# Value passes over other PSUM banks, an eighth place for attention outputs, and loads moved between two DMA queues, in a two-network kernel

## The chip, the cores and the metric

The kernel runs on one core of one Trainium2 chip. The time is device microseconds of one execution, the median of the runs that are shown. Four compute engines have queues of their own and run in the order written for each: TensorE (PE, matrix products into PSUM, with its weight loads shown as PEld), VectorE (DVE), ScalarE (ACT) and GpSimd (POOL). SyncE (SP) issues transfers only. A transfer (DMA) can be issued on the queue of SP or on that of POOL. An instruction that waits holds up everything behind it in its own queue.

## What is computed

A network of two layers (`first_block`) and then a second one (`second_block`), on 512 tokens of width 1024, all in float32. The change touches the first network only. Each of its layers is, cut to what matters:

```python
h = rms_norm(x, g_mix[l])
c_q, c_kv, k_r, qkv_b, qkv_c, gate_logits = jnp.split(h @ w_in[l], IN_SPLITS, axis=-1)
y_a = mla_mixer(c_q, c_kv, k_r, ...)                       # 8 heads, keys and values from a rank-128 latent
y_b = dilated_mixer(rope(q_b), rope(k_b), v_b)             # 3 groups of 4 heads; the groups' outputs are
                                                           # merged with softmax(lse) as weights
y_c = neighbourhood_mixer(q_c, k_c, v_c, rpb[l])           # 8 heads, each looks at a window, with a bias table
gates = sigmoid(gate_logits)
merged = gates[0] * (y_a @ w_pa) + gates[1] * (y_b @ w_pb) + gates[2] * (y_c @ w_pc)
x = x + merged @ w_o[l]
h = rms_norm(x, g_ffn[l])
x = x + (silu(h @ w1[l]) * (h @ w3[l])) @ w2[l]
```

## The kernel before

**Products.** Every float32 operand is split into a high and a low part (`split`, L245: ACT writes the high part at L248, or L251 where there is a scale; DVE the low part at L249 or L252), and a product is three matmuls (`mm3`, L264; in the trace L266 to L268). A weight tile is loaded on SP's queue into `wst` (two places) and split into `whi` and `wlo` (three places each; `weights`, L255).

**PSUM.** Eight banks under four names (L1576): `mm` 3, `S` 2 (attention scores), `T` 2 (transposed probabilities), `O` 1 (attention outputs). Names rotate over their own places, so a product into a bank waits until the readers of its last tenant are done.

**Two streams woven.** Attention is written as short steps (`attn_pair`, L318: scores, transposes at L363, products with the values at L404, and DVE's addition of the two halves at L414, for two heads, a "head pair", at a time). `weave` (L458) puts between these steps a second stream of dense work, the fill, as much of it as the steps' costs times a ratio ask for. The order that results is fixed when the program is built.

**First stage of a layer** (0 to 136 us and 1003 to 1120 us of the trace). `latent` (L771) makes the latent queries and keys, pauses twice (L807 and L817, by the numbers in `PAUSE`, which count fill), takes two column sums with `ones_sum` and roots them (`inv_root`: ACT's square root, then DVE's reciprocal; `rcol` turns the second into columns `rc3`), and writes the latent values to DRAM (`vda`). Its fill is `v_tokens` (L713), the values of all other heads: two passes of 32 products 512 wide and a third 256 wide. The first two take the banks T, T, S, S, and the third two halves of each T. Each result goes out by `v_store` (L740): ACT and DVE scale and split it into `vn`, of which there are two places, and POOL issues the store of `vn` (L743). A layer has 28 such stores, 20 of values and 8 of latent values.

**Attention** (136 to 560 us and 1110 to 1540 us). Fourteen pairs: four latent, then six dilated (three groups of two), then four of neighbourhood attention (nb, units `u` 0 and 1 of two pairs). `v_load` (L745) fetches a pair's values from DRAM into `V` (two places), with one to eight transfers on POOL's queue (L753; eight for nb). An output is collected in a tile `O` of a pool of six places (`obufs`, L1578), which is also used for other tiles of that size. `stat_rows` writes a group's maxima and denominators through a small tile `row` or `row8` to DRAM. After the third dilated group `dil_merge` (L937) loads them (`st`, L940), computes the merge weights, writes these to DRAM (`fd`, L956), loads them back spread over partitions (`RD`, two places, twelve transfers on POOL's queue, L961) and multiplies the six dilated outputs by them (DVE, L963) and adds them up (POOL, L965). Only then are the places of four of these six outputs free.

**The end of attention.** Finished outputs go to DRAM as `yd` and come back by `load_split` (L593: a load on POOL's queue, L595, then a split). The fill of the last nb unit is `first_outputs` (L600) and `first_products` (L614), which multiplies the latent and the dilated outputs by their weights. After the stream, `early_outputs` (L1016) loads and splits the outputs of nb unit 0, and the loop at L651 multiplies all four nb outputs by `wpc`, with `m` and `t` loaded from DRAM (`ry` and `gate`, two places each).

Of the kernel before, what the change touches and what calls it, by code (L numbers as in the profile page):

```python
# [20 lines left out]
S = 512  # L21
# [14 lines left out]
W1 = 2.0  # L36
PAUSE = ((11000, 8000), (9000, 11500))
# [174 lines left out]
class _Net:  # L212
# [105 lines left out]
    def attn_pair(self, scores, nk, mask, v, order, rq=None, wide=False, pre=None, post=None):  # L318
# [9 lines left out]
        def score(j, g):  # L328
            if j == 0 and g == 0:
                c["nmx"] = self.t(self.tp, "nmx", (P, 2, 4), bufs=3)  # L330
                c["den"] = self.t(self.tp, "den", (P, 2, 4), bufs=3)
                c["o"] = self.t(self.tp, "O", (P, S), bufs=self.obufs)
# [166 lines left out]
    def stat_rows(self, stat, order, dst):  # L499
# [3 lines left out]
        if len(order(ps).shape) == 2:  # L503
            nc.tensor.transpose(ps[0:8, 0:P], stat.rearrange("p j b -> p (j b)"), self.ident)
            row = self.t(self.tp, "row8", (8, P), bufs=1)
# [5 lines left out]
        row = self.t(self.tp, "row", (2, S), bufs=1)  # L511
# [54 lines left out]
    def first_layer(self, l, acc, xsrc, emit_x):  # L566
        nc, a = self.nc, self.a
        with ExitStack() as lctx:
# [45 lines left out]
            def first_products():  # L614
# [7 lines left out]
                for n in range(8):  # L622
                    t = self.t(self.tp, "gate", (P, S), bufs=2)
# [18 lines left out]
            with ExitStack() as actx:  # L642
# [70 lines left out]
    def v_tokens(self, win, rc, vd):  # L713
# [3 lines left out]
        for base, units, width, per in ((24, (0, 1), 512, 2), (28, (2, 3), 512, 2), (32, (4,), 256, 4)):  # L717
            if width == 512:
                ps = [self.bank(x) for x in "TTSS"]
            else:  # L720
                ps = [bk[:, i * 256:i * 256 + 256] for bk in [self.bank(x) for x in "TT"] for i in range(2)]
                w = [self.weights(win[base + c]) for c in range(2)]
            for k in range(8) if width == 512 else ():
                if k % per == 0:
                    w = self.weights(win[base + k // per])
                o = slice(k % per * width, (k % per + 1) * width)
# [3 lines left out]
            for tk in range(4):  # L730
                for k in range(8) if width == 256 else ():
                    o = slice(k % per * width, (k % per + 1) * width)
                    self.mm3(ps[tk], self.hh[:, k, sl[tk]], self.hl[:, k, sl[tk]], w[k // per][0][:, o], w[k // per][1][:, o],
                             k == 0, k == 7)
                    yield 330
                for i, u in enumerate(units):
# [918 lines left out]
```

## Time and profile before

| | us |
|---|---|
| median of 3 runs | 2542.53 (2536.6 to 2544.38) |
| profiled execution | 2536.82, its span 2535.0, mean granted TensorE clock 0.962 |
| PE busy | 2366.3 (93% of the span) |
| DVE, ACT, POOL busy | 1571.8 (62%), 1174.7 (46%), 797.8 (31%) |
| first layer, second layer | about 0 to 1005 and 1005 to 1960 |
| second network | about 1960 to 2535 |

The page of the profile gives these shares first, then the span in 40 slices, then the transfers. The granted clock is 1.0 where TensorE runs at 2.4 GHz and 0.5 where it runs at 1.2 GHz; a mean between the two says how the stretch was divided. A wait is put down to the instruction that released it. A line of code can be that of a helper: L248, L249, L266 to L268 are used everywhere, so the name of the tile tells which work it is.

### The profile page before, as it was taken

To read this page: it belongs to the slowest core of one execution; us is meant where nothing else is said; L and a number is where in the kernel's file an instruction comes from. 1 tells how busy PE (TensorE), PEld (TensorE's weight loads), DVE (VectorE), ACT (ScalarE), POOL (GpSimd) and SP (SyncE) were. 2 spreads that over 40 slices of the span, in tenths; PEclk is the share of its full clock that TensorE was granted. 3 is DMA by queue.
4 is the path that set the end of the run, shared out by engine and by line. 5 is a ranking of instruction groups with operands and counts; after the bars stand their busy time and mean duration, and the time that the engine had idled before them with its cause. 6 is when DMAs were issued, how large, how long until landed. Compare 5 with 4: busy or idle time off the path is not lost. (4 is left out here: it accounts for less than half of the span.)

```text
span 2535.0 us, 31781 instructions
## 1 busy us (share of the span) xinstructions
PE 2366.3 (93%) x11200; PEld 1945.8 (77%) x11200; DVE 1571.8 (62%) x2387; ACT 1174.7 (46%) x2072; POOL 797.8 (31%) x953
## 2 busy tenths in 40 slices
PE   7799998789999999889999788999999899979995
PEld 5688887578888888678888577878888788858884
DVE  6477796566444333567878566676533667697666
ACT  5366675344323223356767343423222366435653
POOL 3225466623111100224547633211112122142214
PEclk9899999799999999989999799999999999989997
DMA  5455556556333344355647455687434332224222
GB/s 169 157 174 147 166 143 187 135 175 209 111 99 93 96 130 133 133 172 160 179 127 192 142 157 183 220 282 230 133 109 151 110 109 81 84 91 121 73 78 75
DMA packets 140462, 362.13 MB, mean 143 GB/s; under 512 B 29744, under 2 KB 37200, under 8 KB 140304
## 3 DMA queue, kind: packets, MB, share of 16 engines
q1 hardware_dynamic: 101456, 275.72, 35.5%
q0 software_dynamic: 38848, 84.39, 11.7%
q8 instruction: 88, 1.44, 0.2%
q14 instruction: 70, 0.57, 0.1%
HBM read 286.78 MB, written 45.86 MB: 131 GB/s over the span
## 5 line engine op out<-in xcount | busy, mean ns | idle before, releaser
L248 ACT ACTIVATE whi<-wst 128x1024 fp32r<-128x1024 f32 (+4 forms) x387 | 374.1, 967 | 712.6 <-PE mm L267 256.8
L249 DVE TENSOR_TENSOR wlo<-wst,whi 128x1024 fp32r<-128x1024 f32 (+4 forms) x387 | 460.6, 1191 | 299.7 <-ACT whi L248 291.8
L266 PE MATMUL mm<-hh,whi 128*128 128x512 f32 x1184 | 470.6, 397 | 11.6 <-ACT whi L248 9.0
L268 PE MATMUL mm<-hh,wlo 128*128 128x512 f32 x1184 | 467.2, 395 | 0.5 <-DVE wlo L249 0.3
L267 PE MATMUL mm<-hl,whi 128*128 128x512 f32 x1184 | 465.4, 393 | 0.0
L266 PEld LDWEIGHTS mm<-hh,whi 128*128 128x128 f32 x1184 | 224.1, 189 | 54.2 <-ACT whi L248 9.6
L268 PEld LDWEIGHTS mm<-hh,wlo 128*128 128x128 f32 x1184 | 223.5, 189 | 49.5 <-DVE wlo L249 2.7
L267 PEld LDWEIGHTS mm<-hl,whi 128*128 128x128 f32 x1184 | 224.1, 189 | 43.2 <-issue 0.2
L697 POOL TENSOR_TENSOR s<-s,rf 128x512 f32<-128x512 f32 x44 | 75.8, 1724 | 400.4 <-ACT s L696 400.4
L363 PE MATMUL T<-ident,E 128*128 128x128 f32 x768 | 119.8, 279 | 7.3 <-DVE pl L249 2.8
L339 PE MATMUL S<-qk,qk 128*128 128x512 f32 (+2 forms) x512 | 114.1, 340 | 12.7 <-ACT E L351 6.5
L534 POOL DMA_DIRECT2D ry<-tmp x136 | 67.9, 506 | 168.3 <-ACT tmp L531 109.5
L248 ACT ACTIVATE ph<-T 128x512 fp32r<-128x512 f32 x160 | 95.0, 596 | 53.1 <-PE T L363 49.3
L363 PEld LDWEIGHTS T<-ident,E 128*128 128x128 f32 x768 | 94.8, 143 | 27.7 <-DVE pl L249 4.0
L249 DVE TENSOR_TENSOR pl<-T,ph 128x512 fp32r<-128x512 f32 x128 | 87.3, 683 | 21.9 <-ACT ph L248 21.3
L339 PEld LDWEIGHTS S<-qk,qk 128*128 128x128 f32 x512 | 80.7, 195 | 25.3 <-ACT E L351 8.5
L415 POOL TENSOR_TENSOR O<-O,ll 64x256 f32<-64x256 f32 x80 | 73.5, 919 | 72.1 <-DVE O L414 70.1
L300 POOL TENSOR_TENSOR tmp<-tmp,tmp 128x512 f32<-128x512 f32 x26 | 42.4, 1630 | 170.6 <-ACT tmp L296 159.5
L348 ACT ACTIVATE E<-E,nmx 128x256 f32<-128x256 f32 (+1 forms) x160 | 72.8, 456 | 47.3 <-DVE nmx L346 46.9
L266 PE MATMUL S<-hh,whi 128*128 128x512 f32 x208 | 82.0, 394 | 5.3 <-ACT hh L251 5.3
L268 PE MATMUL S<-hh,wlo 128*128 128x512 f32 x208 | 81.8, 393 | 1.3 <-DVE wlo L249 1.3
L267 PE MATMUL S<-hl,whi 128*128 128x512 f32 x208 | 82.0, 394 | 0.4 <-DVE hl L252 0.4
(626 smaller groups left out, 5595.2 us busy)
## 6 DMA issues: line engine op xcount, KB each, us to landing
wst<-win SPq DMA_DIRECT2D x153, 512.0 KB, 4.0
wst<-w SPq DMA_DIRECT2D x120, 512.0 KB, 3.6
mw<-wada SPq DMA_DIRECT2D x48, 512.0 KB, 4.5
td<-gate SPq DMA_DIRECT2D x48, 256.0 KB, 3.1
vd<-vn POOLq DMA_DIRECT2D x40, 256.0 KB, 2.3
qk<-qk POOLq DMA_DIRECT2D x80, 128.0 KB, 3.1
V<-vd POOLq DMA_DIRECT2D x80, 128.0 KB, 6.4
ry<-tmp POOLq DMA_DIRECT2D x136, 64.0 KB, 3.9
```

The lines of the kernel that those rows point to most:

```text
L248: nc.scalar.activation(hi, src, AF.Copy)
L249: nc.vector.tensor_tensor(lo, src, hi.bitcast(F32), op=ALU.subtract)
L266: mm(out, ah, bh, start=start, stop=False, **kw)
L267: mm(out, ah, bl, start=False, stop=False, **kw)
L268: mm(out, al, bh, start=False, stop=stop, **kw)
L300: self.nc.gpsimd.tensor_tensor(new, acc, sq, op=ALU.add)
L339: nc.tensor.matmul(sp[:, i * nk:(i + 1) * nk], a, b, start=n == 0, stop=n == len(ops) - 1)
L348: nc.scalar.activation(e[:, sl], e[:, sl], AF.Exp, scale=-1.0, bias=m, accum_out=d)
L363: nc.tensor.transpose(tp[:, i * P:(i + 1) * P], e[:, i * P:(i + 1) * P], self.ident)
L415: nc.gpsimd.tensor_tensor(dst, dst, lo, op=ALU.add)
L534: nc.gpsimd.dma_start(out=y[r:r + 32], in_=f[r ^ 32:(r ^ 32) + 32])
L697: nc.gpsimd.tensor_tensor(s, s, r, op=ALU.mult)
```

## The change

Seven edits, all in the first network:

1. **Value passes.** The first pass takes the banks mm, mm, mm, T, the second T, S, S, O, the third two halves of one `mm` bank for each two token tiles. The latent values take `mm` only, where they alternated between `mm` and `O`. `rc` is passed as a function, so that it is looked up when a store needs it.
2. **Pauses and ratio.** `PAUSE` is (31000, 10000) for both layers, and `W1` 1.0 where it was 2.0.
3. **Output places.** `obufs` is 7 where it was 6, and the first dilated output of a layer lies in a place of its own outside that pool (`spare`, the tag `accf`): eight in all. `row8` and `row` become one tile.
4. **Value loads** (`v_load`) are issued on SP's queue, not POOL's: 50 transfers in a layer.
5. **Loads of finished outputs** (`load_split`) too: 8 in a layer.
6. **Last splits in the fill.** `early_outputs` runs inside `first_products`, ahead of its seventh of eight rounds, not after the stream.
7. **Merge loop.** `m` is taken from `tmp` (4 places) and `t` from `O` (7 places).

```diff
-W1 = 2.0
-PAUSE = ((11000, 8000), (9000, 11500))
+W1 = 1.0
+PAUSE = (31000, 10000)
...
-                c["o"] = self.t(self.tp, "O", (P, S), bufs=self.obufs)
+                c["o"] = home() if home else self.t(self.tp, "O", (P, S), bufs=self.obufs)
...
-            row = self.t(self.tp, "row8", (8, P), bufs=1)
+            row = self.t(self.tp, "row", (8, self.roww), bufs=1)[:, 0:P]
...
-        row = self.t(self.tp, "row", (2, S), bufs=1)
+        row = self.t(self.tp, "row", (8, S), bufs=1)[0:2]
...
-                nc.gpsimd.dma_start(out=y, in_=self.yd[i])
+                nc.sync.dma_start(out=y, in_=self.yd[i])
...
-            def first_products():
+            def first_products(early):
...
                 for n in range(8):
+                    if n == 6:
+                        early()
                     t = self.t(self.tp, "gate", (P, S), bufs=2)
...
-                    m = self.t(self.tp, "ry", (P, S), bufs=2)
+                    m = self.t(self.tp, "tmp", (P, S))
                     nc.sync.dma_start(out=m, in_=td[n])
-                    t = self.t(self.tp, "gate", (P, S), bufs=2)
+                    t = self.t(self.tp, "O", (P, S), bufs=self.obufs)
...
-        for base, units, width, per in ((24, (0, 1), 512, 2), (28, (2, 3), 512, 2), (32, (4,), 256, 4)):
-            if width == 512:
-                ps = [self.bank(x) for x in "TTSS"]
-            else:
-                ps = [bk[:, i * 256:i * 256 + 256] for bk in [self.bank(x) for x in "TT"] for i in range(2)]
...
+        for base, units, tags in ((24, (0, 1), ("mm", "mm", "mm", "T")), (28, (2, 3), "TSSO")):
+            ps = [self.bank(x) for x in tags]
...
+        w = [self.weights(win[32 + c]) for c in range(2)]
+        for tk in range(4):
+            if tk % 2 == 0:
+                bk = self.bank("mm")
+            ps = bk[:, tk % 2 * 256:tk % 2 * 256 + 256]
...
-                self.nc.gpsimd.dma_start(out=(v[:, s:s + i + cnt] if cnt > 1 else v[:, s + i]).bitcast(F32), in_=src)
+                self.nc.sync.dma_start(out=(v[:, s:s + i + cnt] if cnt > 1 else v[:, s + i]).bitcast(F32), in_=src)
...
-                ps = self.bank(("mm", "O")[tk % 2])
+                ps = self.bank("mm")
...
+        def spare():
+            return self.fp.tile([P, S], F32, name=f"o{l}", tag="accf")
...
-                groups += self.attn_pair(sc, 256 if g == 0 else P, mask, vf, orders[g], post=post)
+                groups += self.attn_pair(sc, 256 if g == 0 else P, mask, vf, orders[g], post=post,
+                                         home=spare if g + p == 0 else None)
...
-        after[6] = lambda: first_products()
+        after[6] = lambda: first_products(early_outputs)
...
         self.stream(stretches())
-        early_outputs()
...
-            self.obufs = 6
+            self.obufs, self.roww = 7, S
```

What this does to the order of the instructions is shown at three places. In these listings a name carries its number, `A<-B,C` is a result and its inputs, and `x8` stands for eight alike in a row.

**VectorE at the merge of the first layer.** Before, L963 are the merge's multiplications, and the L414 are the first two additions of the first nb pair (its output O_759):

```order
L963 TENSOR_TENSOR O_453_2087<-O_453_2087,RD_812_3839 128x512
L963 TENSOR_TENSOR O_583_2747<-O_583_2747,RD_813_3843 128x512
L963 TENSOR_TENSOR O_672_3184<-O_672_3184,RD_814_3848 128x512
L414 TENSOR_TENSOR O_759_3623<-O_822_3902,O_759_3623 64x32x8
L414 TENSOR_TENSOR O_759_3623<-O_833_3967,O_759_3623 64x32x8
```

Now the multiplications are L976 (the first on the spare place o0) and the same additions write O_758:

```order
L506 COPY row_860_4064<-T_859_4062 8x128
L249 TENSOR_TENSOR ph_856_4056<-T_855_4051,ph_856_4056 128x4x128
L414 TENSOR_TENSOR O_758_3623<-O_832_3967,O_758_3623 64x32x8
L976 TENSOR_TENSOR o0_2087<-o0_2087,RD_811_3839 128x512
L578 TENSOR_TENSOR gate_877_4171<-mm_878_4172,r0_172 128x512
L249 TENSOR_TENSOR wlo_928_4394<-wst_926_4392,whi_927_4393 128x1024
L976 TENSOR_TENSOR O_582_2747<-O_582_2747,RD_812_3843 128x512
L249 TENSOR_TENSOR ph_872_4130<-T_871_4125,ph_872_4130 128x4x128
```

The second addition now stands ahead of the first multiplication, the first addition ten rows above this piece, and the multiplications are no longer in a row.

**ScalarE at the end of the first layer's attention.** Before, O_1000 is the output of the last nb pair and tmp_1110, tmp_1111 hold the loaded outputs of nb unit 0:

```order
L412 ACTIVATE ll_1103_5237<-O_1102_5232 64x256
L413 ACTIVATE O_1000_4764<-O_1102_5232 64x32x8
L248 ACTIVATE qk_1104_5243<-O_1000_4764 128x512
L248 ACTIVATE qk_1106_5247<-tmp_1110_5251 128x512
L248 ACTIVATE qk_1107_5248<-tmp_1111_5255 128x512
```

Now the last pair's output is O_999, and this is what stands at the same place:

```order
L412 ACTIVATE ll_1108_5249<-O_1107_5244 64x256
L413 ACTIVATE O_999_4764<-O_1107_5244 64x32x8
L248 ACTIVATE qk_1109_5255<-O_999_4764 128x512
L248 ACTIVATE whi_1121_5271<-wst_1120_5270 128x512
L579 ACTIVATE gate_1080_5125<-gate_1080_5125 128x512
```

The splits of the loaded outputs (now of tmp_1058 and tmp_1059) stand some thirty rows earlier in that queue, and on TensorE 42 matmuls stand between the last L404 and the first product with `wpc`, where before it followed at once; of these the product's last quarter needs the last pair's output.

**SyncE in the middle of nb unit 0 of the first layer.** V_835 is the values of the fourth nb pair, `td` and `E<-td` are stores and loads of gates. Before, there was no value load here:

```order
L260 DMA wst_959_4568<-wpb 128x256
L633 DMA E_940_4472<-td_27_174 128x512
L633 DMA E_958_4566<-td_27_174 128x512
L633 DMA E_978_4666<-td_27_174 128x512
L260 DMA wst_967_4594<-win 128x1024
L260 DMA wst_972_4636<-wpa 128x512
```

Now:

```order
L260 DMA wst_958_4568<-wpb 128x256
L595 DMA tmp_910_4328<-yd_26_173 128x512
L635 DMA E_957_4566<-td_27_174 128x512
L761 DMA V_835_3993<-vd_29_182 128x1x256 x8
L260 DMA wst_966_4594<-win 128x1024
L635 DMA E_977_4666<-td_27_174 128x512
L260 DMA wst_971_4636<-wpa 128x512
```

Eight value loads, which wait for the last product with the second nb pair's values, now stand ahead of a weight load in one queue.

## Rows read from the trace of the kernel before

**Rows 1.** The page: busy time, share of the span, instructions of each engine.
```profile
PE 2366.3 (93%) x11200; PEld 1945.8 (77%) x11200; DVE 1571.8 (62%) x2387; ACT 1174.7 (46%) x2072; POOL 797.8 (31%) x953
```

**Rows 2.** Stretches: from:to, length, busy PE, PEld, DVE, ACT, POOL, clock, DMA share, GB/s.
```profile
430.00:475.00 45.00, 26.56 (x110) 19.84 (x109) 22.30 (x46) 16.20 (x38) 35.03 (x49) 0.70 0.51 144
...
560.00:575.00 15.00, 9.79 (x35) 7.75 (x34) 6.85 (x11) 4.25 (x8) 2.43 (x2) 0.77 0.42 135
575.00:1010.00 435.00, 435.00 (x1918) 359.74 (x1917) 184.99 (x203) 141.15 (x176) 73.21 (x44) 1.00 0.41 126
...
1410.00:1455.00 45.00, 26.18 (x104) 19.25 (x103) 22.68 (x45) 16.27 (x38) 34.88 (x47) 0.70 0.50 144
```

**Rows 3.** Waits of PE from 430 to 575 us: total, times, longest, in us.
```profile
PE O L404 <- DVE O L414: 12.6, 6, 7.7
...
PE mm L266 <- ACT whi L248: 4.5, 1, 4.5
PE S L339 <- DVE nmx L346: 3.0, 2, 2.2
```

**Rows 4.** Stretches at the lower clock in 430 to 575 us, columns as above.
```profile
438.90:452.60 13.70, 4.64 (x16) 3.56 (x16) 6.14 (x8) 3.76 (x7) 12.18 (x17) 0.50 0.31 101
...
565.20:572.10 6.90, 5.18 (x12) 4.11 (x13) 2.38 (x4) 1.67 (x3) 0.00 (x0) 0.51 0.31 93
sum 41.20, PE 24.70 PEld 18.18 DVE 17.09 ACT 12.80 POOL 27.14; mean PE 6.18 PEld 4.54 DVE 4.27 ACT 3.20 POOL 6.79
```

**Rows 5.** Timeline of DVE at the merge: start, duration, instruction, [idle before <- releaser].
```profile
443.34 2.37 DVE L963 TENSOR_TENSOR O<-O,RD 128x512 f32<-128x512 f32 x1 [4.32 <-DMA RD<-fd]
445.63 0.58 DVE L414 TENSOR_TENSOR O<-O,O 64x256 f32<-64x256 f32 x1
```

**Rows 6.** Timelines of PE and ACT at the end of attention.
```profile
566.92 0.80 PE L266 MATMUL S<-qk,whi 128*128 128x512 f32 x1 [5.21 <-ACT qk L248]
...
566.26 1.13 ACT L248 ACTIVATE qk<-tmp 128x512 fp32r<-128x512 f32 x2
```

**Rows 7.** Transfers issued 470 to 490 us; last row 380 to 600: us to landing.
```profile
V<-vd POOLq DMA_DIRECT2D x8, 128.0 KB, 7.1
wst<-win SPq DMA_DIRECT2D x1, 512.0 KB, 7.0
...
wst<-win SPq DMA_DIRECT2D x11, 512.0 KB, 3.7
```

**Rows 8.** Timelines of SP and ACT: issue of that weight tile, its split.
```profile
480.55 0.33 SPq L260 DMA_DIRECT2D wst<-win  x1
...
487.68 1.06 ACT L248 ACTIVATE whi<-wst 128x1024 fp32r<-128x1024 f32 x1 [6.05 <-DMA wst<-win]
```

**Rows 9.** Waits of PE for value stores: first layer (40 to 136), second (1010 to 1110).
```profile
PE O L266 <- DVE vn L252: 4.0, 1, 4.0
PE T L266 <- DVE vn L252: 3.9, 2, 2.2
...
PE T L266 <- DVE vn L252: 11.0, 4, 6.9
PE O L266 <- DVE vn L252: 6.8, 1, 6.8
```

**Rows 10.** Timeline of POOL: every second store of values, second layer.
```profile
1078.73 0.54 POOL L743 DMA_DIRECT2D vd<-vn  x1 [2.05 <-DVE vn L252]
...
1082.35 0.54 POOL L743 DMA_DIRECT2D vd<-vn  x1 [1.77 <-DVE vn L252]
```

**Rows 11.** Timelines of PE, then DVE, in the second layer's first stage.
```profile
1017.08 0.39 PE L266 MATMUL T<-whi,hh 128*128 128x512 f32 x1
...
1106.47 0.39 PE L266 MATMUL T<-whi,hh 128*128 128x256 f32 x1 [1.25 <-DVE vn L252]
...
1043.45 3.34 DVE L306 RECIPROCAL O<-tmp 128x512 f32<-128x512 f32 x1
```

**Rows 12.** Sum of the lower-clock stretches of the first stages of both layers.
```profile
sum 47.70, PE 36.04 PEld 29.95 DVE 21.68 ACT 16.90 POOL 12.58; mean PE 5.15 PEld 4.28 DVE 3.10 ACT 2.41 POOL 1.80
```

More of the change, by code (lines that the diff above doesn't have):

```diff
@@ L315, in rcol, with attn_pair @@
         return c
-    def attn_pair(self, scores, nk, mask, v, order, rq=None, wide=False, pre=None, post=None):
+    def attn_pair(self, scores, nk, mask, v, order, rq=None, wide=False, pre=None, post=None, home=None):
         nc = self.nc
@@ L716, in v_tokens, with store @@
         sl = [slice(tk * P, (tk + 1) * P) for tk in range(4)]
-        for base, units, width, per in ((24, (0, 1), 512, 2), (28, (2, 3), 512, 2), (32, (4,), 256, 4)):
-            if width == 512:
-                ps = [self.bank(x) for x in "TTSS"]
-            else:
-                ps = [bk[:, i * 256:i * 256 + 256] for bk in [self.bank(x) for x in "TT"] for i in range(2)]
[L722 to L726, printed above, removed]
+        def store(ps, tk, units):
+            for i, u in enumerate(units):
+                self.v_store(ps[:, i * 256:i * 256 + 256], rc()[:, tk:tk + 1], vd[sl[tk], u * 512:u * 512 + 512])
+        for base, units, tags in ((24, (0, 1), ("mm", "mm", "mm", "T")), (28, (2, 3), "TSSO")):
+            ps = [self.bank(x) for x in tags]
+            for k in range(8):
+                if k % 2 == 0:
+                    w = self.weights(win[base + k // 2])
+                o = slice(k % 2 * 512, k % 2 * 512 + 512)
                 for tk in range(4):
@@ L730, in v_tokens @@
             for tk in range(4):
[L731 to L736, printed above, removed]
-                    self.v_store(ps[tk][:, i * 256:i * 256 + 256], rc[:, tk:tk + 1], vd[sl[tk], u * 512:u * 512 + 512])
+                store(ps[tk], tk, units)
+        w = [self.weights(win[32 + c]) for c in range(2)]
[3 more added lines that the diff above has]
+            ps = bk[:, tk % 2 * 256:tk % 2 * 256 + 256]
+            for k in range(8):
+                o = slice(k % 4 * 256, k % 4 * 256 + 256)
+                self.mm3(ps, self.hh[:, k, sl[tk]], self.hl[:, k, sl[tk]], w[k // 4][0][:, o], w[k // 4][1][:, o],
+                         k == 0, k == 7)
+                yield 330
+            store(ps, tk, (4,))
         yield 0
@@ L806, in latent @@
             self.split(ch, cl, ck, self.col(f"g_kv{l}"))
-            yield PAUSE[l][0]
+            yield PAUSE[0]
             r2 = self.inv_root(self.ones_sum(acc), 256, self.eps, self.t(self.tp, "tmp", (P, S)))
@@ L816, in latent @@
             rc3 = self.rcol(r3, "rc3")
-            yield PAUSE[l][1]
+            yield PAUSE[1]
             vd = st["vd"] = self.t(self.dr, "vda", (S, 1024), bufs=1)
@@ L1013, in values @@
         def values():
-            yield from self.v_tokens(win, st["rc"], st["vall"])
+            yield from self.v_tokens(win, lambda: st["rc"], st["vall"])
         def early_outputs():
@@ L1199, in second_net @@
             cp = self.cp = pool("c2")
-            self.obufs = 2
+            self.obufs, self.roww = 2, P
             xt = [x[:, i] for x in [self.t(self.tp, "p" + t, (P, 2, S), bufs=2) for t in "hhll"] for i in range(2)]
```

## The prediction

> **What bounds the kernel now.** I read the page first: PE is busy for 93% of the span, the next engine for 62% [rows 1]. Then the stretches: from 575 to 1010 us PE has work for all of 435.00 us, 1918 matmuls at the full clock, one every 0.227 us [rows 2]. There nothing can be gained, only lost. The time is PE's work, plus PE's waits, plus what it loses when its clock falls to half after a wait. So an edit counts only where PE waits, and that is in two places of each layer. One is the merge and the neighbourhood attention (nb) behind it: from 430 to 475 us PE is busy for 26.56 of 45 us, at a mean clock of 0.70, and from 560 to 575 us for 9.79 of 15; the second layer repeats it 980 us later with 26.18 of 45 [rows 2]. The other is the first stage, where PE waits for value stores: 4.0 and 3.9 us in the first layer, 11.0 and 6.8 in the second [rows 9].
>
> How much is there in the nb part of one layer? The largest entries in the table of PE's waits from 430 to 575 us are 12.6, 4.5 and 3.0 [rows 3] and 5.21 at the end [rows 6], 25.3 in all. Besides, 41.20 us of these stretches run at half clock (1.2 GHz), of which PE is busy for 24.70 [rows 4]; at the full clock that work takes half as long, so 12.4 us are lost. Together some 38 us a layer, 76 in two. In the first stages PE is busy at half clock for 36.04 us [rows 12], 18 us lost.
>
> **The merge and eight places (edit 3).** DVE's multiplication at 443.34 sat 4.32 us for its loaded weights, and the addition L414 of the first nb pair stood behind it in the queue [rows 5]. PE's next product with the values needs the bank that this addition reads, and that is its longest wait, 7.7 us [rows 3]. The additions stood there because the pair's output needed a place that only the merge frees. With eight places the first two nb pairs need none of those: in the new order their additions stand ahead of, and between, the multiplications. Saved: 7.65, and half of the 4.64 us that PE was busy in the slow stretch from 438.9 to 452.6 [rows 4], 2.3: **10 us a layer**. What is late next: the places for two of the split latent outputs still need the merge, but their products stand about fifty matmuls behind PE's old place of waiting, 11 us. Bounds: 0 (the wait moves to these splits whole) and 10.
>
> Behind it lie small waits, mostly between 447 and 475 us: 4.9 us left of the 12.6, 3.0 for L346 [rows 3], and the half clock on the other 14.9 us of work (24.70 less 4.64 and 5.18 [rows 4]), 7.4: 15 us. They come where attention steps stand close together with little dense work between, and the new order still has such a place. I take half, **7.5 a layer**, from bounds of 0 and 15.
>
> **The last splits in the fill (edit 6).** Here PE sat 5.21 us, since the splits of two loaded tiles stood in ACT's queue behind the split of the last pair's output, itself late by a chain over DVE and POOL [rows 6]. Now these splits are done long before, and 42 matmuls, 9.5 us at 0.227, lie between the last L404 and the first product with `wpc`; the last pair's output is due nine matmuls later still. Its chain took from 561.7 to 567.4 (566.26 and 1.13 [rows 6]), so it is hidden. Saved: 5.21 and half of 5.18 [rows 4], **7.8 a layer**, firm.
>
> **Value loads and output loads on SP (edits 4 and 5).** POOL loses 58 issues a layer; it is 31% busy and nothing of PE's waits is its own, so the gain is in the lines above or nowhere. SP gets them, with two costs. A value load waits for the last product with its place's old tenant, and the weight loads behind it wait too. In the new order I looked at every weight tile behind a value load: all but two have over 19 us of PE's work between that product and their first use. The two stand behind the fourth nb pair's eight loads: one with 15 us, and the first with 37 matmuls, at most 8.4 us. It needs 8 issues of 0.33 us [rows 8], its landing and ACT's split of 1.06. With the median landing of 3.7 us that is 7.4, no wait; with the 7.0 us that a tile took beside eight value loads [rows 7], 10.7, a wait of 2.3. Before, the same tile was 4.5 us late [rows 3] for that very reason: it was issued at 480.55 and split at 487.68 [rows 8]. I take **no change** here; bounds 4.5 saved and 2.3 more lost.
>
> The Trainium skill, on the page "DMA: Bandwidth & Descriptors", section "Issuing engines are not separate DMA queues", says that transfers from all issuing engines run on the same 16 DMA engines and interleave, so that issuing from several saves only the issue time. The trace agrees: a tile on SP's queue took 7.0 us, not 3.7, beside loads on POOL's [rows 7]. By that rule this wait stays, as I take it; if separate queues did matter, the sum would be 2.3 a layer worse.
>
> **The value passes (edits 1 and 2).** The second pass no longer waits for the first one's stores. But every store still passes through two `vn` places, and that chain has its own pace: 3.62 us for two stores in the second layer [rows 10], 1.81 each. In the new order the latent stores and those of the second pass stand behind `rc3`, which comes late because of the long pause. For the second layer: the first pass starts at 1017.08 [rows 11] and two passes with their sums are about 195 matmuls, 44 us, to 1061.6. For the root I count 5.5 (the reciprocal alone took 3.34 [rows 11], the square root stands ahead of it and the columns behind): 1067. Twenty stores remain; PE's later products wait for the 12th (1087) and up to the 19th (1100). Before, the wait that answers to it ended at 1106.47 [rows 11]. So 6 us are gained there at best, and PE sits some 18 us in one piece between 1067 and 1087 in place of several pieces. What follows runs at half clock, which takes part of it back. In the first layer the same sum ends within 3 us of the old end. I take **3 a layer**, with bounds of -5 and +7.
>
> **Small edits.** The shared `row` tile adds a wait for the landing of a store that is long done by then. Edit 7: PE has no wait in the merge loop behind 575 us [rows 2], so deeper loads save nothing; they take places that are free by then. Cost 0, and a few us if the early loads meet weight loads on SP. The second network is untouched.
>
> **Sum.** 10 + 7.5 + 7.8 + 0 + 3 = 28.3 a layer, 56.6 in two. The profiled execution took 2536.82 us, which gives **2480**. The median of the runs shown lies 5.7 us (0.2%) above that execution; a median of the new kernel may lie as much above.
>
> **Rivals.**
> *The store chain goes too* (faster): if the stores don't hold PE at all, all waits for `vn` go, 25.7 us [rows 9], and the 18 us at half clock, in place of the 6 taken: 38 more, **2442**. For it: bank waits are what the trace names. Against it: the pace of the `vn` places, which the change leaves alone.
> *The merge still gates* (little gain): the split latent outputs, or the products behind them, wait for the merge's places as the first addition did. Then 10 and 7.5 are lost in both layers: **2515**. For it: twelve `RD` loads through two places, 4.32 us for one of them [rows 5], are unchanged. Against it: the eleven us of work in front.
> *SP's queue starves PE* (slower): a value load that waits for PE holds the weight loads behind it. If a tile comes late as the one in [rows 3] did, PE loses 4.5 and, as behind the wait at the end, 2.6 of half clock: 7. A layer has 14 pairs with value loads. From nine such tiles in both layers on the gain is gone. At half of the 28, 98 lost against 56.6: **2578**. For it: SP waits in order, and eight transfers go ahead of one tile. Against it: 15 us of cover or more for all tiles but one a layer. The skill's same page, section "Queues, rings and completion order", says that each DMA engine takes turns between queue rows packet by packet; by that, a weight tile in the same row as the value loads would come behind all of them, and no run here shows that yet.
> *The change doesn't do what it says* in the first stage: one long wait in place of several and a cold clock behind it, 5 lost in place of 3 gained: **2496**.
>
> **How the numbers follow.** Forecast 0.52, store chain gone 0.13, merge still gates 0.18, first stage worse 0.11, SP starves 0.06. The range goes from 2442 (the store chain gone) to 2522 (merge still gates, and the first stage's 6 not gained), and leaves out about 2 in 10. Faster by over 0.3% (7.6 us, about what a measurement of this kernel can tell from no change) holds in all cases but SP's and the far end of the merge's: 0.88; within 0.3%: 0.06; slower: 0.06.
>
> **What would show it.** Right: no wait of PE for L414 over 2 us near 440 and 1420; no wait at the first product with `wpc`; PE busy for over 36 of the 45 us at the merge; one wait of 15 to 20 us for `vn` in the first stage, with stores 1.8 us apart. Wrong: waits of `mm` L266 for ACT's `whi` behind value loads (SP); a wait for splits `O` from `tmp` in first_products (merge); no wait over 3 us in the first stage (store chain).

## Result and the profile after

| | before | after |
|---|---|---|
| median of the runs, us | 2541.91 (2536.60 to 2544.38) | 2509.99 (2506.84 to 2510.62) |
| profiled execution: span, us | 2535.0 | 2508.9 |

The ratio is 0.9875, 95% interval 0.9857 to 0.9893: 31.9 us less, where 56.6 were forecast. The sign is right and the time lies in the range; the size is a little over half, and it is divided otherwise than the sum had it.

First what came as forecast. The page's line on the engines answers to [rows 1]: PE has 19 us less work time in all (the same matmuls, fewer of them at half clock), and POOL is busy for 74 us less.

```profile
PE 2347.2 (94%) x11200; PEld 1937.8 (77%) x11200; DVE 1561.6 (62%) x2387; ACT 1171.0 (47%) x2072; POOL 724.0 (29%) x837
```

The stretches that answer to [rows 2] are full where they should be (columns as there: from:to, length, busy time of PE, PEld, DVE, ACT and POOL, clock, DMA share, GB/s). The 45 us at the merge hold 37.8 us of PE's work in place of 26.6, and the end of attention has no wait at all. But PE's longest wait in this part now begins at 476 us, just behind that stretch: taken to 490 us, PE is busy for 42.5 of 60 us in place of 36.8, so half of the gain at the merge is gone 15 us later.

```profile
430.00:475.00 45.00, 37.84 (x179) 31.06 (x178) 25.58 (x56) 19.45 (x47) 29.82 (x38) 0.85 0.50 159
560.00:575.00 15.00, 15.00 (x68) 12.43 (x67) 12.62 (x15) 5.80 (x10) 7.82 (x5) 1.00 0.68 218
575.00:1000.00 425.00, 425.00 (x1874) 351.53 (x1873) 176.74 (x195) 136.83 (x169) 65.83 (x39) 1.00 0.39 120
1393.00:1438.00 45.00, 37.74 (x180) 30.97 (x179) 28.83 (x61) 21.81 (x53) 31.97 (x38) 0.85 0.52 171
```

The waits of PE from 380 to 580 us (waiting instruction, its releaser, total, times, longest) show what took the place of [rows 3]. L414 is gone, 0.6 us in place of 12.6. But the wait for a weight tile has grown from 4.5 to 9.9, and the one for `nmx` from 3.0 to 6.1.

```profile
PE mm L266 <- ACT whi L248: 9.9, 1, 9.9
PE S L339 <- DVE nmx L346: 6.1, 2, 5.0
PE T L363 <- DVE row L512: 2.5, 1, 2.5
...
PE O L404 <- DVE O L414: 0.6, 2, 0.4
```

Both are followed back along the timelines (start, duration, instruction, idle time before it and what ended that). In the order SP, ACT, PE, the chain of the 9.9:

```profile
468.69 7.10 SPq L761 DMA_DIRECT2D V<-vd  x8
475.90 1.85 SPq L260 DMA_DIRECT2D wst<-win  x1
...
485.21 1.06 ACT L248 ACTIVATE whi<-wst 128x1024 fp32r<-128x1024 f32 x1 [10.07 <-DMA wst<-win]
...
486.32 0.80 PE L266 MATMUL mm<-hh,whi 128*128 128x512 f32 x1 [9.87 <-ACT whi L248]
```

And of the 5.0, in the order SP, DVE, PE:

```profile
432.78 8.71 SPq L761 DMA_DIRECT2D V<-vd  x8
441.60 2.18 SPq L584 DMA_DIRECT2D td<-gate  x1
...
451.79 0.69 DVE L578 TENSOR_TENSOR gate<-mm,r 128x512 f32<-128x512 f32 x1 [7.64 <-DMA td<-gate]
...
453.21 1.22 PE L339 MATMUL S<-qk,qk 128*128 128x256 f32 x4 [4.97 <-DVE nmx L346]
```

Here it isn't a weight tile that is late but a store: `gate` has two places, the next product can be scaled only when an old one has been stored, and its store stood behind eight value loads on SP. DVE then holds the maxima (`nmx`) that PE wants. Both waits are followed by half clock: the mean granted clock is 0.60 from 448.25 to 465.30 us and 0.58 from 476.45 to 492.60. The second layer repeats them, with 9.7 and 4.7.

In the first stage there is one long wait for `vn` in each layer, 17.35 and 17.25 us (of 22.7 and 20.9 us in four waits each), with stores that follow each other in pairs, 3.63 apart in the first layer (90.10, 93.73 us), which is 1.8 each as in [rows 10].

```profile
101.92 0.77 PE L266 MATMUL mm<-whi,bias 128*128 128x512 f32 x1 [17.35 <-DVE vn L252]
```

### The profile page after: what moved, and what is told of

It is laid out like the page before. It is cut to its first block, busy times and chain, and to the rows that moved or that the text cites. A ratio compares the mean times of both kernels' runs of the same rounds, so it can differ in the third digit from the quotient of the medians.

```text
span 2508.9 us, 31833 instructions
## 1 busy us (share of the span) xinstructions
PE 2347.2 (94%) x11200; PEld 1937.8 (77%) x11200; DVE 1561.6 (62%) x2387; ACT 1171.0 (47%) x2072; POOL 724.0 (29%) x837
## 3 DMA queue, kind: packets, MB, share of 16 engines
q1 hardware_dynamic: 124368, 300.36, 38.2%
## 5 line engine op out<-in xcount | busy, mean ns | idle before, releaser
L267 PE MATMUL mm<-hl,whi 128*128 128x512 f32 x1184 | 468.4, 396 | 0.0
L266 PEld LDWEIGHTS mm<-hh,whi 128*128 128x128 f32 x1184 | 225.4, 190 | 64.8 <-ACT whi L248 20.5
L267 PEld LDWEIGHTS mm<-hl,whi 128*128 128x128 f32 x1184 | 225.5, 190 | 43.7 <-issue 0.2
L339 PE MATMUL S<-qk,qk 128*128 128x512 f32 (+2 forms) x512 | 110.8, 335 | 12.6 <-DVE nmx L346 12.0
L339 PEld LDWEIGHTS S<-qk,qk 128*128 128x128 f32 x512 | 81.1, 196 | 22.4 <-DVE nmx L346 13.2
L267 PE MATMUL S<-hl,whi 128*128 128x512 f32 x208 | 82.7, 398 | 0.0
```

The lines of the kernel that those rows point to most:

```text
L266: mm(out, ah, bh, start=start, stop=False, **kw)
L267: mm(out, ah, bl, start=False, stop=False, **kw)
L339: nc.tensor.matmul(sp[:, i * nk:(i + 1) * nk], a, b, start=n == 0, stop=n == len(ops) - 1)
```

## The experiments

All times are medians, beside a run of the kernel before on the same chip (2539.8 to 2542.2). Runs of the changed kernel reach from 2506.8 to 2510.6. A table of waits is that of one execution, the profiled one. Edits 5 and 7 were not undone by themselves.

**e1_vload_pool: edit 4 undone.**

```diff
-                self.nc.sync.dma_start(out=(v[:, s:s + i + cnt] if cnt > 1 else v[:, s + i]).bitcast(F32), in_=src)
+                self.nc.gpsimd.dma_start(out=(v[:, s:s + i + cnt] if cnt > 1 else v[:, s + i]).bitcast(F32), in_=src)
```

> The changed kernel with edit 4 alone undone: value loads on POOL's queue again. Theory 1 (value loads hold SP's queue, so weight tiles behind them come late): in the changed kernel eight value loads keep SP for 7.1 to 8.7 us, and PE then waits 9.87 us for a weight tile near 476, 4.97 near 448 and 2.48 near 391; with the loads on POOL these fall to 4.5, under 1 and under 1, and their half clock goes: 12 to 18 us a layer less, 2474 to 2488 us in all. Theory 2 (the small waits behind the merge come from the shared row tile and the merge's own chain, whatever queue loads the values): within 6 us of the changed kernel's 2510, and the waits for row and nmx stay. Theory 3 (POOL becomes late with the loads, its additions and stores wait behind them): slower than 2510.

Measured: 2501.51 us, ratio 0.9846 [0.9829, 0.9863]; 8.5 less than the changed kernel, a quarter to a third of what theory 1 said. The 8.5 is a rough size: the two intervals just overlap (the changed kernel's begins at 0.9857), the four runs here reach from 2495.1 to 2507.7, and the profiled one is the slowest. PE waits 2.4 for tiles in place of 9.9 (theory 1 had 4.5); but L414 is back, and `nmx`, which theory 1 had under 1, has stayed. Waits of PE from 380 to 580 us:

```profile
PE O L404 <- DVE O L414: 7.7, 5, 2.6
PE S L339 <- DVE nmx L346: 4.8, 2, 3.8
...
PE mm L266 <- ACT whi L248: 2.4, 2, 2.0
```

What holds L414 at the merge can be read from the timelines, in the order POOL, DVE:

```profile
450.65 1.87 POOL L1013 TENSOR_TENSOR bias<-bias,maskc 128x768 f32<-128x768 f32 x1
452.43 1.31 POOL L978 TENSOR_TENSOR o<-o,O 128x512 f32<-128x512 f32 x1
...
450.61 3.68 DVE L976 TENSOR_TENSOR O<-O,RD 128x512 f32<-128x512 f32 x1
454.41 0.58 DVE L414 TENSOR_TENSOR O<-O,O 64x256 f32<-64x256 f32 x1
```

The merge's multiplication in front of L414 lasts 3.68 us, where most of its kind take 0.65 to 0.70. It runs beside two operations of POOL and ends 0.56 us after the second; L414 follows, and PE's longest wait for it, 2.65, ends there. The four shorter ones make up the other 5.

So the queue of the value loads chooses which wait stands there. Theory 1 has the mechanism of the changed kernel right; that the time behind it is free to take is wrong.

**e2_before_vload_sp: the kernel before with edit 4 alone** (the same line, other way round).

> The kernel before with edit 4 alone: only the value loads move to SP's queue. Theory 1: its weight tiles come late as in the changed kernel, 8 to 16 us a layer lost: 2558 to 2574 us, with waits of PE for whi of over 7 us in the neighbourhood part. Theory 2 (the queue does not matter): within 6 us of the kernel before.

Measured: 2528.49, ratio 0.9943 [0.9922, 0.9964]: faster by 12.5, where theory 1 had 16 to 32 slower and the other no change. Both fell by the time. The late tile costs 5.0 in the first layer and 9.1 in the second, where it was 4.5 in each, so the wait over 7 us that theory 1 named came in one layer. But L414 costs PE 1.3 and 3.0 in place of 12.6 and 12.2. So moving the loads is worth something by itself, through the merge, and the prediction had nothing for that.

**e4_early_back: edit 6 undone.**

```diff
-        after[6] = lambda: first_products(early_outputs)
+        after[6] = lambda: first_products(lambda: None)
...
         self.stream(stretches())
+        early_outputs()
```

> The changed kernel with edit 6 alone undone: the last splits after the stream again. The prediction's step (7.8 us a layer, called firm) expects 15.6 us more than the changed kernel, some 2526, and PE's wait of 5 us at the first product with wpc back in each layer. Rival: in the changed kernel the chain of the last pair is no longer late at that point, so the wait is under 1 us and the time the same.

Measured: 2533.28, ratio 0.9971 [0.9960, 0.9982]: edit 6 is worth 23.3, more than the 15.6 of the sum. The wait at the first product with `wpc` is back, and longer than before [rows 6]:

```profile
564.44 0.80 PE L266 MATMUL S<-qk,whi 128*128 128x512 f32 x1 [6.64 <-ACT qk L248]
```

PE is busy for 6.16 us at half clock beside and behind it (stretch, columns as above):

```profile
560.30:570.60 10.30, 6.16 (x15) 4.81 (x16) 3.50 (x5) 1.90 (x4) 0.85 (x1) 0.50 0.64 203
```

So 6.64 and half of 6.16 make 9.7 in the first layer, and the second has a wait of 6.49; that is some 19 of the 23.3.

**e3_values_back: edits 1 and 2 undone.** The two loops of `v_tokens`, `PAUSE`, `W1` and the banks of the latent values are those of before:

```diff
-W1 = 1.0
-PAUSE = (31000, 10000)
+W1 = 2.0
+PAUSE = ((11000, 8000), (9000, 11500))
...
-        for base, units, tags in ((24, (0, 1), ("mm", "mm", "mm", "T")), (28, (2, 3), "TSSO")):
+        for base, units, width, per in ((24, (0, 1), 512, 2), (28, (2, 3), 512, 2), (32, (4,), 256, 4)):
```

> The changed kernel with edits 1 and 2 undone: value passes, pauses and weave as in the kernel before. The prediction's term is 3 us a layer (bounds -5 and 7): 2516 us, 6 more than the changed kernel. By the two traces the first stage of the first layer was some 4 us a layer shorter after the change: 2518. Rival: what the first stage gains is taken back where the neighbourhood part begins, as in e6_vn_in_E: 2507 to 2513.

Measured: 2523.22, ratio 0.9921 [0.9908, 0.9935]: 13.2 more than the changed kernel, about twice what the first two expectations had (6 and 8), and the rival fell. I add PE's idle time and half of the time that it was busy at half clock, stretch by stretch. From 20 to 330 us that makes 33.8 here, 28.6 in the changed kernel and 31.8 before; in the second layer 27.7, 26.8 and 26.6. So the first stage accounts for 6 of the 13. The rest is in the nb part (by the same sum 40.3 against 38.2 from 330 to 650 us, and 41.4 against 37.0 from 1290 to 1640), where the other order has its own late load: ACT waits 10.59 us for an output that edit 5 loads through SP, behind eight value loads; L414 stands behind that on DVE, and PE waits 6.9 for it. In the order SP, ACT:

```profile
399.48 9.70 SPq L755 DMA_DIRECT2D V<-vd  x8
...
410.62 2.86 SPq L595 DMA_DIRECT2D tmp<-yd  x3
...
422.32 0.63 ACT L248 ACTIVATE nq<-tmp 128x512 fp32r<-128x512 f32 x1 [10.59 <-DMA tmp<-yd]
```

**e5_six_places: edit 3 undone**, and **e17_six_and_pool: edits 3 and 4 undone** (e5's edit and e1's).

```diff
-            self.obufs, self.roww = 7, S
+            self.obufs, self.roww = 6, S
...
-                                         home=spare if g + p == 0 else None)
+                                         home=None)
```

> The changed kernel with edit 3 undone: six places for attention outputs, and the first dilated output has no place of its own. The prediction's terms for it are 10 a layer and 7.5 for the small waits behind the merge: 2530 to 2545 us, with PE's wait of 7 us for L414 at the merge back. Rival: in the changed kernel the late weight tiles hold PE at the same place, so the merge's wait lies beside them and the time is within 6 us of 2510.

> The changed kernel with edits 3 and 4 both undone: six places, and value loads on POOL's queue. With the changed kernel (both, 2510), e5_six_places (4 alone, 2508) and e1_vload_pool (3 alone, 2501) it makes a square of the two. The prediction's theory (places are what the additions at the merge wait for) expects the wait of 7 us for L414 back in both layers: 2522 to 2536, so edit 3 pays 20 to 35 where edit 4 is absent. Rival (the merge's loads through POOL's queue, behind the value loads there, are what is late; the places pay little): the nb part costs what it costs in e1_vload_pool, 2497 to 2508.

Measured: 2508.40 (0.9871 [0.9858, 0.9885]) and 2527.59 (0.9947 [0.9932, 0.9961]). With the changed kernel and e1 they make a square:

| median, us | value loads on POOL | value loads on SP |
|---|---|---|
| six places | 2527.6 (e17) | 2508.4 (e5) |
| eight places | 2501.5 (e1) | 2510.0 (changed) |

So e5 came out as its rival said, and e17's time as the prediction's theory said. Alone, edit 3 is worth 26.1 and edit 4 19.2. Together they are worth 17.6: neither adds anything to the other. Waits of PE from 380 to 580 us, e17's first line and then two of e5:

```profile
PE O L404 <- DVE O L414: 7.2, 4, 4.1
```

```profile
PE mm L266 <- ACT whi L248: 5.5, 2, 3.9
...
PE O L404 <- DVE O L414: 0.4, 1, 0.4
```

L414 costs PE 7.2 and 7.7 with the loads on POOL, 0.4 and 0.6 with them on SP, whatever the number of places. So in these four kernels the wait that the prediction gave to the places hangs on the queue. (It is not so everywhere: with the loads on SP and eight places L414 costs 12.3 in e3 and 5.1 in e11, behind late loads.) With the loads on SP, six places even have the smaller waits for tiles and `nmx`, 5.5 and 1.6 where eight have 9.9 and 6.1. The places pay 26 where the queue is POOL's, but not by taking that wait away whole: its longest piece falls from 4.1 to 2.6. In the second layer the total falls from 8.6 to 5.9.

**e10_small_staging: big weight tiles ahead of the value loads.** The small tiles `wpa` and `wpb` are loaded into the idle places of `vn`, so that the big tiles find a staging place earlier and stand ahead of the last two sets of loads.

```diff
-        st = self.t(self.wp, "wst", (P, 1024), bufs=2)
+        st = self.t(self.tp, "vn", (P, S), bufs=2) if small else self.t(self.wp, "wst", (P, 1024), bufs=2)
```

> The changed kernel, value loads still on SP's queue, with one edit: the tiles of wpa and wpb are loaded into the two places of vn, which nothing else uses at that time, in place of the weights' two staging places. The big win tiles then stand ahead of the last two sets of eight value loads on SP's queue, not behind them; the third set (near 391 us) still has three win tiles behind it. Theory 1 (PE waits for weight tiles that stand behind value loads): PE's waits of 9.87 us near 476 and 4.97 near 448, and the half clock behind them, go, and the one of 2.48 near 391 stays: 8 to 16 us a layer, 2478 to 2494 us in all. Rival (e1_vload_pool moved the loads off SP's queue altogether and took only 8 us in two layers off; as there, the nb part then waits for something else as long): no tile of win is late, but the waits for nmx, O and the merge's loads grow, and the time is 2498 to 2510.

Measured: 2507.14, ratio 0.9859 [0.9846, 0.9873], as the rival said. No big tile is late near 450 and 480; the store of `gate` still is. Timelines of SP, then DVE:

```profile
432.76 9.59 SPq L761 DMA_DIRECT2D V<-vd  x8
442.44 1.52 SPq L584 DMA_DIRECT2D td<-gate  x1
...
452.67 0.69 DVE L578 TENSOR_TENSOR gate<-mm,r 128x512 f32<-128x512 f32 x1 [8.73 <-DMA td<-gate]
```

PE's wait for `nmx` behind it is 5.9, and 3.6 have come at L404 near 486 us, where DVE's L414 stands behind the split of a small tile, `wpa`, whose load is issued behind the fourth set of value loads. Theory 1 in its narrow form, the big weight tiles alone, falls: whatever is behind the eight loads comes late.

**e18_both_queues: the loads of several parts dealt to both queues.**

```diff
-                self.nc.sync.dma_start(out=(v[:, s:s + i + cnt] if cnt > 1 else v[:, s + i]).bitcast(F32), in_=src)
+                eng = self.nc.gpsimd if len(pp) > 1 and i % 2 else self.nc.sync
+                eng.dma_start(out=(v[:, s:s + i + cnt] if cnt > 1 else v[:, s + i]).bitcast(F32), in_=src)
```

> The changed kernel with the value loads of several parts dealt to SP's and POOL's queue in turn. If what delays the weight tiles is that they stand behind eight loads on one queue, four loads on it delay half as long: the wait of 9.87 near 476 falls to 3 to 5, that of 4.97 to 0 to 2, and with POOL's queue only half as loaded the merge's loads are not late: 2488 to 2500. If the delay comes from the megabyte that the sixteen engines have to move, whichever queue it comes from, the waits stay over 7 and 4, and the time within 6 us of 2510.

Measured: 2510.98, ratio 0.9883 [0.9868, 0.9897], no change. The tile's wait is about halved, nearly as the first theory said, and four loads held SP's queue for 2.3 to 2.9 us in the first layer, where eight took 7.1 to 8.9. But waits for L414 have come, 8.0 in all (4.0 of it near 405 us, behind a load of the merge's statistics, `st`), and `nmx` stays at 5.8. The time is the second theory's, though its waits over 7 and 4 are not. Waits of PE from 380 to 580 us:

```profile
PE mm L266 <- ACT whi L248: 5.3, 1, 5.3
PE O L404 <- DVE O L414: 4.0, 4, 1.7
PE T L363 <- DVE O L414: 4.0, 1, 4.0
```

**e6_vn_in_E and e11_staging_and_e: more places for the value stores.** e6 is e1 with value stores and attention's `E` in five places of one tag; e11 is e10 with the stores taking the two places of `vn` and the three of `E` in turn (attention keeps three). First e6, then e11:

```diff
-        vn = self.t(self.tp, "vn", (P, 4, 2, 64), F32R, bufs=2)
+        vn = self.t(self.tp, "E", (P, 4, 2, 64), F32R, bufs=self.ebufs)
...
-            e = c["e", j, g] = self.t(self.tp, "E", (P, S), bufs=3)
+            e = c["e", j, g] = self.t(self.tp, "E", (P, S), bufs=self.ebufs)
```

```diff
-        vn = self.t(self.tp, "vn", (P, 4, 2, 64), F32R, bufs=2)
+        self.vi = (getattr(self, "vi", -1) + 1) % 5
+        tag, k = ("E", 3) if self.vi % 2 == 0 else ("vn", 2)
+        vn = self.t(self.tp, tag, (P, 4, 2, 64), F32R, bufs=k)
```

> The kernel of e1_vload_pool with one more edit: value stores take their tile from the same set of places as the attention weights E, five places in all in place of two for vn and three for E. If the pace of the stores through two places (1.81 us each) makes PE's wait of 17.3 us for vn in each first stage, the stores now follow each other at the pace of POOL's issue, 0.54 us each, the wait falls to 4 to 8 us a layer and the time by 16 to 28 us against e1_vload_pool. If the wait is due to the late column tile rc3 or to the second pass's position instead, the wait stays over 14 us and the time within 6 us of e1_vload_pool.

> e10_small_staging with one more edit: value stores take the two places of vn and the three of E in turn. In e6_vn_in_E five places took the wait of 17.3 us for vn down to 6.9 and 7.5, but only 4 us of the time by the medians (10 by the profiled spans), since a wait of 9.2 us for the merge stood in the second part of each layer. If that wait came from the five places that attention's E tiles had there (they have three here), the first stages now give 10 us a layer against e10_small_staging: 16 to 24 us. If the first stage's gain is taken back by the later part whatever the places of E, it is 0 to 10.

Measured: 2497.50 (0.9830 [0.9816, 0.9843]) and **2484.01** (0.9772 [0.9759, 0.9785]). The wait for `vn` falls to 6.9 and 6.8 in the first layer, so the two places made most of the 17.3, as e6's first expectation had it. e11's line of the waits from 40 to 136 us:

```profile
PE mm L266 <- DVE E L252: 7.6, 2, 6.8
```

By the sum of idle time and half clock, the first stages of e11 (20 to 330 and 990 to 1290 us) lose 16.5 and 17.0, against 27.3 and 26.7 in e10: 20.5 less, where the medians are 23.1 apart and the profiled spans 17.0. So the gain is made there, as e11's first expectation said. e6 gains as much there, but 4 by the medians against e1 (10 by the profiled executions) where 16 to 28 were expected, since its nb part has one wait of 9.2 at L267 for an output's split, behind the merge. e11 is the best version run: 26 us below the changed kernel.

**e13_best and e19_best_pool: edits 3 and 4 undone in e11.** e13 has six places and, in the room that leaves, `row8` and `row` apart as before; e19 has the value loads on POOL's queue.

```diff
-            row = self.t(self.tp, "row", (8, self.roww), bufs=1)[:, 0:P]
+            row = self.t(self.tp, "row8", (8, P), bufs=1)
...
-        row = self.t(self.tp, "row", (8, S), bufs=1)[0:2]
+        row = self.t(self.tp, "row", (2, S), bufs=1)
```

> e11_staging_and_e with edit 3 undone (six places) and, in the room that leaves, a row tile of its own for each kind of statistics, as before the change. If edit 3 pays nothing where the value loads are on SP's queue, as e5_six_places says, and the waits for row (2.6 and 1.8 to 2.4 us) come from DVE standing behind a late weight tile, the time is that of e11_staging_and_e, 2478 to 2490, and the waits for row stay. If the shared row tile makes the waits for row, they go, and the time is 2466 to 2478. If edit 3 pays its 10 a layer once the tiles are no longer late, 2495 to 2510.

> e11_staging_and_e (2484) with edit 4 alone undone: value loads on POOL's queue. In the changed kernel undoing edit 4 gave 8 less, because eight value loads in front of weight tiles on SP's queue cost more than POOL's shorter queue gave. If that also holds where the last two sets of loads no longer stand in front of the big tiles, 2470 to 2480. If the small weights' own staging had taken the cost away, edit 4 pays here, since POOL's queue (value loads, then the merge's loads and additions) is what is late: 2488 to 2505, with waits of PE for L414 and nmx between 430 and 460 us of over 8 in all.

Measured: 2503.38 (0.9853 [0.9837, 0.9869]) and 2496.67 (0.9829 [0.9815, 0.9842]). So in e11 edit 3 pays 19.4, 9.7 a layer (the row tiles were not tried apart by themselves), as e13's third expectation had it, and edit 4 pays 12.7, as e19's second had it. In the changed kernel they were worth -1.6 and -8.5. The waits for `row` stay in e13, so the shared tile does not make them. PE's 9.1 there stands behind ACT, which waits 9.81 us for a reloaded output (`tmp<-yd`), a load on SP's queue. Waits of PE from 380 to 580 us in e13, then in e19:

```profile
PE mm L266 <- ACT qk L248: 9.1, 1, 9.1
...
PE T L363 <- DVE row L506: 4.3, 2, 3.8
PE T L363 <- DVE row L512: 2.8, 1, 2.8
```

```profile
PE mm L267 <- DVE O L249: 9.9, 2, 9.4
PE O L404 <- DVE O L414: 6.3, 5, 1.7
```

In e19 the 9.4 is the merge again. DVE stands idle for a load of the merge's weights, 3.25 us, the instruction itself is recorded with 4.15 where most of its kind take 0.65 to 0.70, and the split that PE wants is behind it. It begins beside two operations of POOL and ends 0.56 us after them (442.98). In the order POOL, DVE:

```profile
439.37 3.61 POOL L1015 TENSOR_TENSOR bias<-bias,maskc 128x768 f32<-128x768 f32 x2
...
439.39 4.15 DVE L978 TENSOR_TENSOR O<-O,RD 128x512 f32<-128x512 f32 x1 [3.25 <-DMA RD<-fd]
443.46 0.68 DVE L249 TENSOR_TENSOR O<-tmp,nq 128x512 fp32r<-128x512 f32 x1
```

Attention's `E` has three places in e19 and five in e6, and both have this wait. So it does not come from the five places, as e11's first expectation supposed; what e6 and e19 share, and e11 has not, are the value loads on POOL's queue.

## Why the prediction was right in sign and short by half

The 24.7 us that are missing can be read off in one order of the edits. From the kernel before to e17, edits 1, 2, 5, 6 and 7 together take 14.3, where the sum had 21.6. From e17 to e1, edit 3 takes 26.1 where it had 35. From e1 to the changed kernel, edit 4 costs 8.5 where it had 0. That is 7.3, 8.9 and 8.5 short. In the other order, edit 4 ahead of edit 3, edit 4 takes 19.2 and edit 3 nothing (1.6 more). That the time lies in the range is in part luck: its upper end was set by the rival in which the merge still gates, and that did not happen.

**Value loads and output loads on SP: the step that failed.** "I take no change here; bounds 4.5 saved and 2.3 more lost" a layer. Edit 4 costs 8.5 in the changed kernel (2501.5 without it), 4.3 a layer, and pays 12.5 in the kernel before. Without that edit the gain is 40.4, still 16.2 short of the 56.6, so the step is a part of the miss and not all of it. Three things in it were wrong.

The size. For the one tile that was named, eight issues of 0.33, a landing of 3.7 to 7.0 and a split of 1.06 made 7.4 to 10.7. The rows above show the eight issues at 7.10, the tile's own at 1.85, 7.46 from there to the split, and the split at 1.06, 17.5 in all. The 0.33 of [rows 8] was the issue of one weight tile on a short queue; the issues, priced at 2.6, took 8.95 with the tile's own. PE ran dry at 476.45, 7.8 after the loads began; the cover was priced at 8.4, so that part held, and the difference is the wait of 9.87.

What was counted. Every weight tile behind a value load was followed, but not the stores and reloads on the same queue. The stores of `gate` behind the third nb set cost 5.0, and in e3 the reload that edit 5 itself put there cost a wait of 6.9. The sentence that named the rival, SP waits in order, had it; its price counted tiles alone.

What it does to the merge. The loads leave POOL's queue, and L414 no longer holds PE. The step had "the gain is in the lines above or nowhere". It is in those lines: the square shows that edits 3 and 4 pay for the same lost time there. In e11, where the big tiles no longer stand behind the last two sets, each of them undone alone costs, 19.4 and 12.7.

The Trainium skill's rule, on the page "DMA: Bandwidth & Descriptors", section "Issuing engines are not separate DMA queues", that issuing from several engines saves only the time to initiate, which it calls usually small beside the transfer, was quoted for taking no change. Here the initiating was 7.10 and 1.85 us beside 7.46 to the split. That time is not small, and it stands in front of all else on that queue.

**The merge, 10 a layer, and the small waits behind it, 7.5.** L414's wait did go, and the 45 us at the merge hold 37.8 us of work, as forecast. But in the changed kernel undoing the eight places changes nothing (2508.4 against 2510.0). Where the loads are on POOL they pay 13 a layer, in e11 9.7. The value was near; its cause was half wrong, as L414 follows the queue in the square and not the places. Nor was the load the whole of it: in [rows 5] the multiplication that L414 stood behind took 2.37 where the two ahead of it took 0.69 and 0.68, and the prediction had nothing for that. The failing is in the sum: 10, 7.5 and 0 were added as if the edits acted on separate waits.

**The last splits in the fill, 7.8, called firm.** The mechanism held and the size was low: 11.7 a layer by e4. The 7.8 took the wait as it was before the change, 5.21 with half of 5.18; without edit 6 the new order would have had 6.64 with half of 6.16, 9.7. The other 2 a layer were not traced. By the sum of idle time and half clock they lie in the nb part too: it loses 10.1 more from 330 to 650 us and 11.6 more from 1290 to 1640.

**The value passes, 3 a layer.** One wait of 18 us and stores 1.81 apart were forecast; 17.35, 17.25 and 1.8 came. (The sum's 1061.6 is 1061.1 by its own terms, which changes nothing behind it.) PE's loss in the first stages fell by 3.2 in the first layer and rose by 0.2 in the second: 3 in all in place of 6, within the bounds. Undoing the edits costs 13.2, half of it in the nb part, by another order.

**Small edits, 0.** PE's waits for `row`, 0.4 before, are 2.5 (near 391) and 1.3 now. The first comes from DVE, which stands 6.26 us behind a weight tile's split: SP's queue again. e13, with the tiles apart, has them too; so has e1, with the loads on POOL (2.5 near 411), and that one was not followed.

**The rivals.** The store chain goes: no, it holds PE for 17.3. The merge still gates, at 2515: near in time, but not by that mechanism, as L414 takes 0.6 and the splits of outputs (`mm` L267) 0.5. SP's queue starves PE: right in kind and place, for two sets of loads a layer in place of seven, which is why the time did not go to 2578. It had a chance of 0.06, since only its large form was priced.

**What stays open.** The waits in the nb part of e1 still come to some 20 us a layer with no late tile; of these only the longest for L414 was followed back. Edits 5 and 7 may cost something: edits 1 and 2 undone cost 13.2 and edit 6 undone 23.3, yet these five together take only 14.3 ahead of edits 3 and 4. Either they work only with edits 3 and 4 in place, or edit 5 or 7 takes part of it back; no run divides these. Why an issue on SP stretches was not tried either.

## What to carry to other kernels

When a transfer moves to another queue, list everything that will stand behind it there, stores and reloads as well as weight tiles, and for each the in-order engine that waits for it. Price the issue of a burst from a burst, not from one issue on a short queue. Two edits that relieve the same stretch are not to be added: price the second with the first in place.

## What the runs showed of the hardware

A load issued on SP's queue was not always 0.33 us. The 92 loads of value tiles take the following there, and on POOL's queue in the kernel before (nanoseconds: least, median, most):

```profile
L761 SPq DMA_DIRECT2D V<-vd x92: 390/538/2412, 228.8 to 1444.3; - x92
```

```profile
L753 POOL DMA_DIRECT2D V<-vd x92: 677/677/834, 226.0 to 1463.8; - x92
```

On POOL the time of one is nearly constant. On SP it grows within a burst. In each of the eight bursts of eight loads of 128 KB in the changed kernel the first three issues took 0.51 to 0.55 us (one took 1.02), the last three 0.87 to 2.41; the eight together took 6.9 to 8.9 (up to 11.5 in e2), against 5.4 on POOL, and the issue behind them up to 2.18. Four loads (e18) took 2.2 to 3.3. I had not expected that the queue with the shorter single issue is the slower one for a burst.

DVE's multiplications of the merge (128x512, both inputs in SBUF) took 0.65 to 0.70 us, or much longer: 2.37 in the kernel before, 3.12 in e17, 3.68 in e1, 4.15 in e19. In these five traces, the changed kernel's with them, each one over 0.7 us runs beside a TENSOR_TENSOR of POOL and ends 0.54 to 0.56 us after it, or after the last where several follow at once. That it waits for POOL is read from these times; no run moved POOL's operations.
